# Moving the low products of each half chunk of weights behind the high products of the next half chunk

## The chip, the cores and the metric

The kernel runs on one core of one Trainium2 chip. The metric is the device time of one execution in microseconds (us). The engines are named as the profile names them: PE (TensorE, the matrix products), PEld (its weight loads), DVE (VectorE), ACT (ScalarE), POOL (GpSimd), SP (SyncE, which issues most of the DMAs here). "L201" is line 201 of the kernel before.

## The reference

One layer of a hybrid encoder block on a sequence of 256 tokens with 2048 channels, all in float32. Cut to what matters:

```python
mod = silu(c) @ W_ada + b_ada                        # six vectors of 2048
h = rms_norm(x) * (1 + scale_m) + shift_m
proj = h @ w_in                                       # 2048 x 18512: mLSTM q,k,v,o; GDN q,k,v,z; merge gates
h_a = bidirectional(mlstm_chunkwise, ...)             # 4 heads
o_b = bidirectional(gated_delta_chunkwise, ...)       # 16 heads
y_a = (sigmoid(a_o) * rms_norm(h_a)) @ w_branch_a
y_b = (rms_norm(o_b) * silu(b_z)) @ w_branch_b
x = x + gate_m * ((g_a * y_a + g_b * y_b) @ w_out)
hf = rms_norm(x) * (1 + scale_f) + shift_f
gt, up = split(hf @ w_gate_up)                        # 2048 x 11264
x = x + gate_f * ((silu(gt) * up) @ w_down)           # 5632 x 2048
return rms_norm(x)
```

Nearly all of the work is a product of 256 tokens with a large matrix of weights, each weight being used once.

## The kernel before

**Three products for one.** The large products are taken with operands of type fp32r, and each operand is split in two: a high part, which is the value written as fp32r, and a low part, which is the value minus the high part. A product x·w is then computed as xh·wh + xl·wh + xh·wl. The first two products need only the high part of the weights (in this document: the *high products*), the third needs the low part (the *low products*). The activations are split once and kept (hh and hl, hfh and hfl, and so on). The weights are split as they come in.

**Jobs.** Two generators make all of these products. `fjob` (names b and a) multiplies one block of 2048 x 128 weights; the weights are the stationary operand, and 256 tokens stream past them. `tjob` (names z, v, o, ma, mb, yb, ya, o again for the output projection, gt, up, d) makes 512 output columns for both halves of the tokens; the tokens are the stationary operand, and 512 columns of weights stream past them. A chunk of weights, 1 MB, is brought by one DMA of SP into a tile `raw`. It is converted in two halves: ACT writes `wh` (L155, L180), then DVE writes `wl = raw - wh` (L156, L181). The tiles raw, wh and wl have three buffers each, which all jobs share, and so do the loads of `ada`, 1 MB each, which DVE reduces to the vectors of `mod` (L124) between other work.

**One half chunk on PE.** In `tjob` a half chunk is two blocks of 128 rows times two halves of the tokens, with three products each: twelve products of 128x512. In `fjob` it is eight blocks with three products each: 24 products of 128x256. Before the change the three products of one block follow each other: L199, L200, L201 (L159, L160, L161 in `fjob`), and the third is the low product.

**What sets the order.** The program is written as generators that are interleaved by hand: `fill(n)` advances a list of waiting jobs by n steps, a step being one half chunk, and `stream` and the tables `after` and `last` say how many steps are put between two steps of the gated-delta-rule chain (`gdn_phase2`), so that PE has work while DVE and ACT finish a link of that chain. The links that the prediction speaks of: L685 writes p, DVE makes pt of it (L686), L694 uses pt; then L707, L708 and L719 in the same way. A scheduler then orders the instructions of each engine by this written order and by its own idea of when operands and buffers are ready; a few are marked to stay in written order. Every engine then runs its own list strictly in order, and waits where an operand is missing. A tile's buffer can be written again once its last reader is done: so `wh` is free after the half chunk's last high product, `wl` after its last low product, and `raw` after both halves have been converted.

**Stages, by the time of the span:** to 137 us the modulation and the first 16 column blocks (not split, L507); from 137 to 1000 us the jobs z, v, mb, o, ma, a and b beside the gated delta rule; to 1226 us the mLSTM with yb and ya; to 1334 us the output projection (o again, from the weights `wo`); to 1360 us the second norm with the first gate job; then the gate and up jobs to 1811 us, and the down jobs (d).

## Time and profile before

| | before |
|---|---|
| median of 3 runs | 2050.77 us (2050.05 to 2060.24) |
| the profiled execution | 2056.24 us, its span 2054.3 us |
| PE busy | 1968.2 us (96%) |
| DVE busy | 1394.8 us (68%) |
| ACT busy | 1054.0 us (51%) |
| products | 10374 |
| DMA | 485.64 MB, mean 236 GB/s |

The span is the time from the first to the last instruction that the profile holds; 1.9 us of the execution lie around it. The profiled execution is one run, 5.5 us above the median. A row of the view of waits reads "who waited, at which line, for which engine's which line: us in total, how often, the longest". A row of the timeline has the start in us from the span's beginning, the duration, the engine, the line, what was written from what, and in brackets the idle time before it with what ended it. In the rows by stretch the busy time of each engine stands with the number of its instructions, and then the share of full speed that TensorE's clock was granted.

### The profile page before, as it was taken

The numbers are of one execution on the slowest core, as the hardware profiler recorded it, in microseconds if no ns is written. First come the engines' busy times: TensorE is split into PE (matmuls) and PEld (weight loads), VectorE is DVE, ScalarE is ACT, GpSimd is POOL, SyncE is SP. The second block draws the span as 40 slices with busy tenths as digits, with TensorE's granted clock in tenths as the row PEclk, the third lists the DMA queues.
The fourth block names the chain that finished last, engine by engine and source line by source line (L and its number), as shares of the span: only waits on it lengthen the run. The fifth ranks groups of instructions, "written<-read, shape, count | busy, mean of one in ns | idle before, by whom it ended". The sixth has DMA issues, their size and how long they took to land.

```text
span 2054.3 us, 27035 instructions
## 1 busy us (share of the span) xinstructions
PE 1968.2 (96%) x10374; PEld 1707.0 (83%) x10374; DVE 1394.8 (68%) x2059; ACT 1054.0 (51%) x1584; POOL 106.1 (5%) x205
## 2 busy tenths in 40 slices
PE   8999989999998899999999999889999999999998
PEld 6777779988987898899878787678888888888886
DVE  5787777786888588765667778766656665555554
ACT  3147547856774677466443443364444444444443
POOL 0002210010101010100200000000000000000000
PEclk9999999999999999999999999999999999999999
DMA  9986664566765565666987578756766766555654
GB/s 400 420 321 211 173 216 146 173 190 221 240 224 178 194 207 211 232 247 241 361 295 263 211 264 315 271 184 240 255 243 245 254 238 221 192 204 204 205 203 143
DMA packets 78962, 485.64 MB, mean 236 GB/s; under 512 B 10585, under 2 KB 15969, under 8 KB 24433
## 3 DMA queue, kind: packets, MB, share of 16 engines
q1 hardware_dynamic: 63360, 450.95, 60.9%
q0 software_dynamic: 8160, 17.88, 4.0%
q10 hardware_dynamic: 7314, 15.10, 1.9%
q8 instruction: 81, 1.33, 0.3%
q14 instruction: 47, 0.39, 0.0%
HBM read 467.07 MB, written 16.82 MB: 236 GB/s over the span
## 4 chain that ended last, share of the span: by engine, by line
PE 67%; DVE 13%; DMA 11%; ACT 5%; issue 3%; POOL 1%; ACTq 0%; SPq 0%; DVEq 0%; POOLq 0%
PE acc_up L201 4%; PE acc_up L199 4%; PE acc_up L200 4%; PE acc_d L200 4%; PE acc_d L201 4%; PE acc_d L199 4%; PE acc_gt L200 3%; PE acc_gt L201 3%; PE acc_gt L199 3%; DMA ra<-ada 3%; PE acc_b L161 2%; PE acc_b L159 2%; PE acc_b L160 2%; DMA ada<-ada 2%; PE acc_yb L201 1%
## 5 line engine op out<-in xcount | busy, mean ns | idle before, releaser
L181 DVE TENSOR_TENSOR wl_d<-raw_d,wh_d 128x1024 fp32r<-128x1024 f32 x88 | 107.8, 1225 | 109.1 <-ACT wh_d L180 109.1
L181 DVE TENSOR_TENSOR wl_up<-raw_up,wh_up 128x1024 fp32r<-128x1024 f32 x88 | 107.7, 1225 | 100.4 <-ACT wh_up L180 100.4
L159 PE MATMUL acc_b<-hh,wh_b 128*128 128x256 f32 x576 | 164.1, 285 | 5.8 <-ACT wh_b L155 5.8
L181 DVE TENSOR_TENSOR wl_gt<-raw_gt,wh_gt 128x1024 fp32r<-128x1024 f32 x88 | 107.8, 1225 | 83.2 <-ACT wh_gt L180 83.2
L161 PE MATMUL acc_b<-hh,wl_b 128*128 128x256 f32 x576 | 161.7, 281 | 2.0 <-DVE wl_b L156 2.0
L124 DVE SCALAR_TENSOR_TENSOR ada<-ada,crow 128x2048 f32<-128x2048 f32 x64 | 146.4, 2287 | 25.0 <-DMA ada<-ada 24.8
L160 PE MATMUL acc_b<-hl,wh_b 128*128 128x256 f32 x576 | 160.4, 279 | 0.0
L180 ACT ACTIVATE wh_d<-raw_d 128x1024 fp32r<-128x1024 f32 x88 | 92.9, 1056 | 127.9 <-PE acc_d L200 119.2
L180 ACT ACTIVATE wh_gt<-raw_gt 128x1024 fp32r<-128x1024 f32 x88 | 92.9, 1056 | 118.6 <-PE acc_gt L200 71.0
L180 ACT ACTIVATE wh_up<-raw_up 128x1024 fp32r<-128x1024 f32 x88 | 92.9, 1055 | 108.9 <-PE acc_up L200 78.2
L199 PE MATMUL acc_gt<-wh_gt,hfh 128*128 128x512 f32 x352 | 135.4, 385 | 0.0
L200 PE MATMUL acc_gt<-wh_gt,hfl 128*128 128x512 f32 x352 | 134.7, 383 | 0.1
L201 PE MATMUL acc_gt<-wl_gt,hfh 128*128 128x512 f32 x352 | 133.7, 380 | 0.0
L199 PE MATMUL acc_up<-wh_up,hfh 128*128 128x512 f32 x352 | 133.5, 379 | 0.0
L201 PE MATMUL acc_up<-wl_up,hfh 128*128 128x512 f32 x352 | 133.5, 379 | 0.0
L200 PE MATMUL acc_up<-wh_up,hfl 128*128 128x512 f32 x352 | 133.5, 379 | 0.0
L200 PE MATMUL acc_d<-wh_d,ffl 128*128 128x512 f32 x344 | 131.0, 381 | 0.0
L199 PE MATMUL acc_d<-wh_d,ffh 128*128 128x512 f32 x344 | 131.0, 381 | 0.0
L201 PE MATMUL acc_d<-wl_d,ffh 128*128 128x512 f32 x344 | 130.5, 379 | 0.0
L507 PE MATMUL first<-x,raw 128*128 128x256 f32 x512 | 114.5, 382 | 7.4 <-ACT x L500 6.8
L159 PEld LDWEIGHTS acc_b<-hh,wh_b 128*128 128x128 f32 x576 | 112.5, 195 | 6.4 <-ACT wh_b L155 6.3
L507 PEld LDWEIGHTS first<-x,raw 128*128 128x128 f32 x512 | 96.1, 190 | 25.8 <-ACT x L500 12.4
(369 smaller groups left out, 5275.9 us busy)
## 6 DMA issues: line engine op xcount, KB each, us to landing
ada<-ada SPq DMA_DIRECT2D x64, 1024.0 KB, 5.0
raw_gt<-wgu SPq DMA_DIRECT2D x44, 1024.0 KB, 5.0
raw_up<-wgu SPq DMA_DIRECT2D x44, 1024.0 KB, 4.9
raw_d<-wd SPq DMA_DIRECT2D x44, 1024.0 KB, 4.9
raw_b<-winb SPq DMA_DIRECT2D x36, 1024.0 KB, 5.4
ra<-ada SPq DMA_DIRECT2D x32, 1025.0 KB, 15.7
raw<-win SPq DMA_DIRECT2D x16, 1024.0 KB, 14.5
raw_z<-wint SPq DMA_DIRECT2D x16, 1024.0 KB, 5.8
```

What stands on the lines that cost most here:

```text
L124: V.scalar_tensor_tensor(raw, raw, 1.0, row_c[:, :D], ALU.mult, ALU.mult, accum_out=mod[:, c0 + b : c0 + b + 1])
L159: PE.matmul(o, wh[:, k], both(hh, kk).rearrange("p a b -> p b a"), start=kk == 0, stop=False)
L160: PE.matmul(o, wh[:, k], both(hl, kk).rearrange("p a b -> p b a"), start=False, stop=False)
L161: PE.matmul(o, wl[:, k], both(hh, kk).rearrange("p a b -> p b a"), start=False, stop=kk == KB - 1)
L180: order(S.activation(wh, raws[u][:, k0 : k0 + 2], AF.Copy), early)
L181: order(V.tensor_tensor(wl, raws[u][:, k0 : k0 + 2], wh.bitcast(F32), ALU.subtract), early)
L199: order(PE.matmul(ps[t], tok(xh, kk, t), turns(wh[:, k]), start=kk == 0, stop=False), early and steps > 1)
L200: PE.matmul(ps[t], tok(xl, kk, t), turns(wh[:, k]), start=False, stop=False)
L201: PE.matmul(ps[t], tok(xh, kk, t), turns(wl[:, k]), start=False, stop=kk == last)
L507: PE.matmul(first[o], raw[:, o], x[:, b], start=b == 0 and o % 2 == 0, stop=b == KB - 1 and o % 2 == 1)
```

## The change

The products stay the same, each with the same operands into the same accumulator; their order on PE changes. A half chunk now issues its high products first and puts its low products on a list. The list is emptied down to one entry after the next half chunk's high products, so that the low products of half n stand behind the high products of half n+1. At the end of a job the list is emptied wholly: the last half's high products are followed by the low products of the last two halves. In `fjob`, which has two halves, the order becomes high, high, low, low. The last chunk of the jobs that end token half by token half (`by_token`) has all its high products first and then its low ones. DVE's and ACT's instructions are the same; the scheduler's order of them shifts.

```diff
@@ fjob
+        late = []
         for k0 in range(0, KB, 8):
             ...
             S.activation(wh, raw[:, k0 : k0 + 8], AF.Copy)
             V.tensor_tensor(wl, raw[:, k0 : k0 + 8], wh.bitcast(F32), ALU.subtract)
+            def lows(k0=k0, wl=wl):
+                for k in range(8):
+                    PE.matmul(o, wl[:, k], both(hh, k0 + k).rearrange("p a b -> p b a"), start=False, stop=k0 + k == KB - 1)
+
             for k in range(8):
-                kk = k0 + k
-                PE.matmul(o, wh[:, k], both(hh, kk).rearrange("p a b -> p b a"), start=kk == 0, stop=False)
-                PE.matmul(o, wh[:, k], both(hl, kk).rearrange("p a b -> p b a"), start=False, stop=False)
-                PE.matmul(o, wl[:, k], both(hh, kk).rearrange("p a b -> p b a"), start=False, stop=kk == KB - 1)
+                for i, x in enumerate((hh, hl)):
+                    PE.matmul(o, wh[:, k], both(x, k0 + k).rearrange("p a b -> p b a"), start=k0 + k + i == 0, stop=False)
+            late.append(lows)
+            while len(late) > (not k0):
+                late.pop(0)()
@@ tjob
         for n, (u, k0) in enumerate(todo):
             wh, wl = made.pop(0) if made else halves(u, k0)
-            for k in range(2):
-                kk = 4 * u + k0 + k
-                for t in range(2):
-                    order(PE.matmul(ps[t], tok(xh, kk, t), turns(wh[:, k]), start=kk == 0, stop=False), early and steps > 1)
-                    PE.matmul(ps[t], tok(xl, kk, t), turns(wh[:, k]), start=False, stop=False)
+            kt = [(4 * u + k0 + k, k, t) for k in range(2) for t in range(2)]
+
+            def lows(kt=kt, wl=wl):
+                for kk, k, t in kt:
                     PE.matmul(ps[t], tok(xh, kk, t), turns(wl[:, k]), start=False, stop=kk == last)
+
+            for kk, k, t in kt:
+                order(PE.matmul(ps[t], tok(xh, kk, t), turns(wh[:, k]), start=kk == 0, stop=False), early and steps > 1)
+                PE.matmul(ps[t], tok(xl, kk, t), turns(wh[:, k]), start=False, stop=False)
+            late.append(lows)
+            while len(late) > (n < len(todo) - 1):
+                late.pop(0)()
@@ by_token
-                    wh, wl = (turns(a[:, k % 2]) for a in w[k // 2])
+                    wh = turns(w[k // 2][0][:, k % 2])
                     PE.matmul(ps[t], tok(xh, kk, t), wh, start=False, stop=False)
                     PE.matmul(ps[t], tok(xl, kk, t), wh, start=False, stop=False)
-                    PE.matmul(ps[t], tok(xh, kk, t), wl, start=False, stop=kk == last)
+                for k in range(4):
+                    kk = last - 3 + k
+                    PE.matmul(ps[t], tok(xh, kk, t), turns(w[k // 2][1][:, k % 2]), start=False, stop=kk == last)
```

What the built programs show at three places (the line numbers of the changed kernel differ: L206 is the low product of `tjob`, L209 and L210 its high products, L164 and L160 the high and the low products of `fjob`, L708 is the old L694, L666, L670 and L671 the old L652, L656 and L657, L187 the old L181).

PE, a merge-gate job (ma), chunk 2, second half; the pair of numbers after "ma" in a weight's name is the chunk and the half. Before:

```order
L200 MATMUL acc_ma_1_3458<-wh_ma_2_0_3774,hl 128x512
L201 MATMUL acc_ma_1_3458<-wl_ma_2_0_3775,hh 128x512
L199 MATMUL acc_ma_0_3457<-wh_ma_2_2_3796,hh 128x512
L200 MATMUL acc_ma_0_3457<-wh_ma_2_2_3796,hl 128x512
L201 MATMUL acc_ma_0_3457<-wl_ma_2_2_3797,hh 128x512
L199 MATMUL acc_ma_1_3458<-wh_ma_2_2_3796,hh 128x512
```

With the change:

```order
L206 MATMUL acc_ma_1_3458<-wl_ma_1_2_3749,hh 128x512
L209 MATMUL acc_ma_0_3457<-wh_ma_2_2_3792,hh 128x512
L210 MATMUL acc_ma_0_3457<-wh_ma_2_2_3792,hl 128x512
L209 MATMUL acc_ma_1_3458<-wh_ma_2_2_3792,hh 128x512
L210 MATMUL acc_ma_1_3458<-wh_ma_2_2_3792,hl 128x512
...
L206 MATMUL acc_ma_0_3457<-wl_ma_2_0_3771,hh 128x512
L206 MATMUL acc_ma_1_3458<-wl_ma_2_0_3771,hh 128x512
```

The first low product of half 2_2 was the third product of that half; now the eight high products of 2_2 are followed by the low products of 2_0, and those of 2_2 stand behind the high products of 3_0.

PE, the first pair of heads of the gated delta rule, between the two links L685 and L694, filled by the first half of a b job. Before:

```order
L159 MATMUL acc_b_0_2141<-hh,wh_b_0_0_2144 128x256
L160 MATMUL acc_b_0_2141<-hl,wh_b_0_0_2144 128x256
L161 MATMUL acc_b_0_2141<-hh,wl_b_0_0_2145 128x256
L694 MATMUL p_0_0_2172<-R,pt_0_0_2131 128x32 x4
L159 MATMUL acc_b_0_2141<-hh,wh_b_0_8_2187 128x256
```

With the change:

```order
L164 MATMUL acc_b_0_2137<-hl,wh_b_0_0_2140 128x256
L708 MATMUL p_0_0_2160<-R,pt_0_0_2127 128x32 x4
L164 MATMUL acc_b_0_2137<-hh,wh_b_0_8_2175 128x256
L164 MATMUL acc_b_0_2137<-hl,wh_b_0_8_2175 128x256
...
L160 MATMUL acc_b_0_2137<-hh,wl_b_0_0_2141 128x256 x8
L160 MATMUL acc_b_0_2137<-hh,wl_b_0_8_2176 128x256 x8
```

Where 24 products stood between the two links, 16 stand now; the eight low products moved behind the second half, whose step holds 32 products now instead of 24.

DVE, just ahead of that place, where the blocks of the inverse arrive (cg) and R is made of them. Before:

```order
L652 STREAM_TRANSPOSE cg_1960<-cg_1960 128x512
L656 TENSOR_SCALAR R<-cg_1960,cst 128x256
L181 TENSOR_TENSOR wl_o_2_0_2115<-raw_o_2_2112,wh_o_2_0_2114 128x1024
L657 SCALAR_TENSOR_TENSOR R<-cg_1960,cst,R 128x256
...
L156 TENSOR_TENSOR wl_b_0_0_2145<-raw_b_0_2142,wh_b_0_0_2144 128x1024
```

With the change:

```order
L666 STREAM_TRANSPOSE cg_1956<-cg_1956 128x512
L670 TENSOR_SCALAR R<-cg_1956,cst 128x256
L671 SCALAR_TENSOR_TENSOR R<-cg_1956,cst,R 128x256
L670 TENSOR_SCALAR R<-cg_1956,cst 128x256
L187 TENSOR_TENSOR wl_o_2_0_2111<-raw_o_2_2108,wh_o_2_0_2110 128x1024
...
L157 TENSOR_TENSOR wl_b_0_0_2141<-raw_b_0_2138,wh_b_0_0_2140 128x1024
```

The low part of that half of o moved behind the first pair of instructions that make R, and on PE its low products moved behind the b jobs of this pair of heads.

More of the change, by code (lines that the diff above doesn't have):

```diff
@@ L184, in tjob @@
         todo = [(u, k0) for u in range(len(chunks)) for k0 in (0, 2)]
-        made = []
+        made, late = [], []
         for i, q in enumerate(todo[:early]):
```

## The prediction

> **What bounds the kernel now.** I read the engines' shares first, then the stretches, then who PE waited for, then the timeline around the longest of those waits.
>
> ```profile
> PE 1968.2 (96%) x10374; PEld 1707.0 (83%) x10374; DVE 1394.8 (68%) x2059; ACT 1054.0 (51%) x1584; POOL 106.1 (5%) x205
> ```
>
> PE is busy for 1968.2 of 2054.3 us, so a change of order, which leaves the number of products as it is, can only touch the 86 us between, and what the products themselves lose when the clock drops. Where those 86 us lie is told by the stretches (PE, PEld, DVE, ACT, POOL, then the granted clock and the DMA's share):
>
> ```profile
> 137.00:300.00 163.00, 152.40 (x673) 125.59 (x672) 130.04 (x268) 99.93 (x154) 29.87 (x55) 0.97 0.65 202
> 300.00:620.00 320.00, 305.59 (x2150) 279.75 (x2149) 246.33 (x496) 228.26 (x431) 33.62 (x67) 0.99 0.61 197
> 1226.00:1334.00 108.00, 96.04 (x408) 76.71 (x406) 84.20 (x104) 42.05 (x61) 0.00 (x0) 0.96 0.81 302
> 1360.00:1811.00 451.00, 450.94 (x2120) 392.22 (x2119) 268.57 (x248) 203.30 (x216) 0.00 (x0) 1.00 0.66 236
> ```
>
> In the gate and up jobs PE is never idle (450.94 of 451.00), so that fifth of the kernel has nothing to win. The idle time is in the mixed stages: 10.6 us from 137 to 300, 14.4 us from 300 to 620, and 12.0 us in the output projection. PE's waits on the jobs' operands, and on two links of the gated-delta chain (in total, how often, the longest):
>
> ```profile
> PE acc_o L201 <- DVE wl_o L181: 8.3, 5, 3.3
> PE acc_v L201 <- DVE wl_v L181: 5.1, 5, 2.4
> PE acc_z L201 <- DVE wl_z L181: 4.4, 6, 1.2
> PE acc_ma L201 <- DVE wl_ma L181: 3.7, 2, 2.0
> PE acc_a L161 <- DVE wl_a L156: 2.7, 3, 1.5
> PE acc_b L161 <- DVE wl_b L156: 2.0, 4, 0.8
> PE acc_mb L201 <- DVE wl_mb L181: 0.3, 1, 0.3
> PE acc_b L159 <- ACT wh_b L155: 5.8, 3, 2.8
> PE acc_o L199 <- ACT wh_o L180: 4.0, 5, 1.9
> PE acc_z L199 <- ACT wh_z L180: 2.6, 3, 1.9
> PE p L719 <- DVE pt L708: 2.2, 3, 1.0
> PE p L694 <- DVE pt L686: 2.2, 3, 1.1
> ```
>
> The first seven rows are what the change aims at: the low part of the weights is late, 26.5 us in 26 waits. The next three, 12.4 us in 11 waits, are waits on the high part, which the change leaves in place. One of the first kind, close up:
>
> ```profile
> 451.17 0.38 PE L199 MATMUL acc_ma<-wh_ma,hh 128*128 128x512 f32 x1
> ...
> 455.06 1.06 ACT L180 ACTIVATE wh_ma<-raw_ma 128x1024 fp32r<-128x1024 f32 x1 [1.50 <-PE acc_ma L200]
> 455.30 0.38 PE L200 MATMUL acc_ma<-wh_ma,hl 128*128 128x512 f32 x1
> 456.08 0.40 DVE L631 TENSOR_TENSOR utmp<-uu 64x240 f32<-64x240 f32 x1
> 456.40 1.21 DVE L181 TENSOR_TENSOR wl_ma<-raw_ma,wh_ma 128x1024 fp32r<-128x1024 f32 x1
> 457.67 0.48 PE L201 MATMUL acc_ma<-wl_ma,hh 128*128 128x512 f32 x1 [1.99 <-DVE wl_ma L181]
> ```
>
> From 451.17 to 455.30 PE starts a product every 0.217 us (20 products, 19 steps). At 455.30 it has done the first two products of half 2_2, and the third needs a low part that DVE, busy inverting, begins at 456.40. The other high products of this half could have run, for their operand is there. From start to start the stall costs 2.37 us instead of 0.22, that is 2.15: 0.16 more than the 1.99 of the row, because the idle time counts only from the modelled end of the product before.
>
> **The change part by part.** *The cover.* A half chunk's eight high products take 8 x 0.217 = 1.7 us. Behind the change a low part may come one such block later without PE stopping, in mid-job. Of the 26.5 us I take off:
>
> - 3.9 us, three waits in the output projection. There the loads set the pace, not DVE:
>
> ```profile
> ACT wh_o L180 <- DMA raw_o<-wo: 31.5, 8, 6.1
> 1264.10 2.36 DVE L181 TENSOR_TENSOR wl_o<-raw_o,wh_o 128x1024 fp32r<-128x1024 f32 x2 [1.46 <-ACT wh_o L180]
> L201 PE MATMUL acc_o<-wl_o,mgh 128*128 128x512 f32 x120 | 46.8, 403 | 4.4 <-DVE wl_o L181 3.9
> ```
>
> - 2.1 us, two waits of z, in a stretch in which DVE has 21.80 of 23 us of work, so that PE only reaches the next late operand sooner:
>
> ```profile
> 137.00:160.00 23.00, 21.80 (x42) 1.00 0.57 200
> 148.08 0.70 PE L201 MATMUL acc_z<-wl_z,hh 128*128 128x512 f32 x2 [0.83 <-DVE wl_z L181]
> 152.18 0.70 PE L201 MATMUL acc_z<-wl_z,hh 128*128 128x512 f32 x2 [1.24 <-DVE wl_z L181]
> ```
>
> - 3.3 us, the longest wait of o, priced by itself below.
> - 2.0 us, the four of b: the same job also waits for its high part (5.8 us in the eighth row), so the high products that should cover are not there.
> - 1.0 us, the parts of the longest v (2.4) and ma (2.0) waits beyond the 1.7 us of cover.
> - 0.8 us: the last half of a job has only the four low products before its own as cover, 4 x 0.217 = 0.9 us, and one ma wait of 1.68 us stands there.
>
> 13.4 us are left, in 16 waits (26 less 3, 2, 1 and 4), each with its 0.16 us beside: 13.4 + 2.6 = 16.0 us. The bounds are nothing (PE meets the same lag a block later) and the whole, 26.5 + 26 x 0.16 = 30.7 us.
>
> *The 3.3 us of o* end at the first pair of heads:
>
> ```profile
> 305.74 0.71 DVE L652 STREAM_TRANSPOSE cg<-cg 128x512 f32<-128x512 f32 x1 [7.26 <-DMA cg<-inv_d]
> 307.88 0.48 PE L201 MATMUL acc_o<-wl_o,hh 128*128 128x512 f32 x1 [3.33 <-DVE wl_o L181]
> 308.29 2.00 ACT L155 ACTIVATE wh_b<-raw_b 128x1024 fp32r<-128x1024 f32 x2
> 312.64 0.36 PE L159 MATMUL acc_b<-hh,wh_b 128*128 128x256 f32 x1
> ```
>
> DVE's list stands behind a DMA (cg) for 7.26 us, and the low part of o behind that. With the change PE goes on to the link L685, which waits for R, and then to b, whose high part is there when ACT's first conversion ends, 308.29 + 1.0 = 309.3. Before, b began at 312.64. 3.3 us earlier, less the four low products still owed (0.9): 2.4 us. Bounds: 0 and 3.3.
>
> *The clock.* Behind such stalls the rows show the granted clock at half for 3.4 or 6.8 us (the windows chosen to fit):
>
> ```profile
> 219.50:226.30 6.80, 6.56 (x19) 5.57 (x20) 3.69 (x12) 3.04 (x8) 0.40 (x1) 0.50 0.73 145
> 226.30:233.10 6.80, 6.80 (x28) 5.04 (x27) 3.26 (x4) 2.11 (x2) 0.00 (x0) 1.00 0.57 212
> 458.50:461.80 3.30, 3.30 (x9) 2.59 (x8) 3.20 (x7) 0.60 (x1) 0.08 (x1) 0.50 0.94 308
> ```
>
> At full clock 28 products begin in 6.8 us, at half clock 19, and 9 in 3.3 us: 6.8 x (1 - 19/28) = 2.2 us lost behind the stall of v at 218, and 3.3 - 9 x 6.8/28 = 1.1 us behind that of ma at 457.67. I take 2 of these 3.3 us as won, since another wait stands just before the first one. Bounds: 0 and 3.3.
>
> The Trainium skill (TensorE: Matmul & The Clock Gate, section "HAM oscillation — how this bites in real kernels") states that idle gaps of PE up to about 3.4 us do not drop the clock. By that rule these 2 us would not be won and the gain would be 2 us less; the trace disagrees, since the row at 458.50 stands at 0.50 behind 1.99 us of idle time.
>
> *The chain's cover.* The first half of a b job between L685 and L694 loses its eight low products. Products of `fjob` begin 0.11 us apart:
>
> ```profile
> 312.83 0.28 PE L160 MATMUL acc_b<-hl,wh_b 128*128 128x256 f32 x1
> 312.94 0.28 PE L161 MATMUL acc_b<-hh,wl_b 128*128 128x256 f32 x1
> ```
>
> So the cover falls from 24 x 0.11 = 2.6 to 1.8 us. Where PE waited there already, three times (L694, 2.2 us), the wait grows by 0.9 each: 2.6 us lost. The later step holds 32 products, and of the three waits at L719 the first, up to 1.0, shrinks by 0.9. At the last group's first pair the filling between the second and third application of the inverse shrinks from nine products of 128x512 to one, 1.7 us, of which I count 1.2. Together 2.6 + 1.2 - 0.9 = 2.9 us lost. Bounds: 0.9 won (DVE comes earlier everywhere) and 8 links x 0.9 + 1.7 = 8.9 lost.
>
> *Buffers.* `wh` comes free earlier by the low products that no longer stand before its last reader; `wl` is freed one half later, 12 x 0.217 = 2.6 us, and `raw` with it where DVE then has to wait for a buffer. In mid-job two of three low buffers hold the waiting halves. I cost it at nothing: where loads are late, PE has used up what it had, and the row at 1264.10 shows DVE making both low parts (2.36 us) as soon as ACT is done, with buffers free. Bounds in the third rival. The jobs of 1360 to 1811 stay at nothing, since no operand is late there.
>
> The sum: 16.0 + 2.4 + 2.0 - 2.9 = 17.5 us. The profiled execution took 2056.24 us (span 2054.3 and 1.9 around it), which gives 2038.7; against the median of the runs, 2050.77, it gives **2033 us**.
>
> **Rivals.** *The lag only moves.* DVE is late because its list is full for a stretch (130.04 of 163 us, 21.80 of 23 at its start). The cover then pays once per stretch and not once per wait: the stretches of z and v, ma, z with a, o with a make about five, 5 x 1.7 = 8.5 us, less the chain's 2.9: some 6 us, 2045 us, within what a measurement can tell from no change (0.5%, about 10 us). For it: the waits of z come in a row. Against it: over each long stretch DVE has a fifth of its time free, and most waits stand alone.
>
> *The chain loses what the jobs win.* All eight links stall (7.2 and 1.7 us), and each new stall brings a piece of half clock like that at 458.50 (1.1 us): 8.9 + 8 x 1.1 = 17.7 us against 20.4 won: 2048 us. Against it: five of the eight links show no wait, so their cover had something to spare.
>
> *Buffers held longer.* If a low buffer kept for one more half delays raw's release and so the next load by 2.6 us, the 11 waits on high parts (12.4 us, loads already late) grow by 2.6 each: 28.6 us against 17.5 won, 11 us slower: 2062 us. It decides from the point at which DVE waits for a buffer and no longer for ACT before it writes a low part, in stages where the loads are just in time. For it: b jobs run while another job is paused with a low part pending, which leaves them two buffers. Against it: the row at 1264.10.
>
> That the change does not do what it says is excluded by the order: the low products stand behind the next half's high ones.
>
> **How the numbers follow.** My forecast 0.57; the lag only moves 0.23; the chain 0.05; buffers 0.13; the last 0.02 for other shifts of the scheduler that cost time. Faster by over 0.5% (below about 2040) only in the first: 0.57; within 0.5% in the second and third: 0.28; slower 0.15. The forecast's own range runs from the whole of the cover with nothing lost, 2050.8 - 30.7 - 3.3 + 2.9 = 2020, to 2040. The range that should hold the time 8 times in 10 takes in both cases of no change and the start of the slower one: 2019 to 2055.
>
> **What would show it.** Right: the seven rows of PE behind DVE's low parts fall from 26.5 to about 9 us, mostly in the output projection; no stall at 457.67, and no half clock behind it; L694 waits about 2.6 us longer; 1360 to 1811 unchanged. The forecast is wrong if waits on wh grow by what the waits on wl lose (the lag moved, or late loads), or if ACT's waits on loads grow by some 2.6 us each.

## The result, and the profile after

The changed kernel takes 2062.64 us (median of 20 runs, 2056.23 to 2072.60) against 2054.22 us of the kernel before on the same chip (20 runs, 2046.72 to 2060.24). The ratio is 1.0045, with an interval of 1.0033 to 1.0057: 9.2 us slower. That lies within the 0.5% that the prediction set as the bound of "no change", but it is clear of zero, and far from the 17.5 us that were forecast as won.

The engines, in the profiled execution of the changed kernel (span 2070.6 us, the execution 2072.6, which is the slowest of its 20 runs; so its stages may be longer than the typical ones):

```profile
PE 1975.9 (95%) x10374; PEld 1720.2 (83%) x10374; DVE 1392.5 (67%) x2059; ACT 1040.5 (50%) x1578; POOL 106.1 (5%) x205
```

PE idles 94.7 us, where it idled 86 before. The view by stretches, cut at the stages: up to the first product of yb, then the output projection, then from its end to that of the first gate job. First the three rows of the kernel before, then those of the changed one. The columns are the bounds, the length, PE, PEld, DVE, ACT, POOL, the granted clock, the DMA's share and GB/s:

```profile
0.00:1016.90 1016.90, 961.37 (x5742) 849.53 (x5743) 751.25 (x1366) 593.29 (x1039) 104.00 (x201) 0.98 0.69 240
1225.60:1328.70 103.10, 94.51 (x401) 75.42 (x399) 81.33 (x96) 39.49 (x53) 0.00 (x0) 0.97 0.85 316
1328.70:1365.50 36.80, 27.84 (x130) 22.61 (x130) 23.92 (x40) 26.23 (x47) 0.00 (x0) 0.95 0.33 115
```

```profile
0.00:1011.70 1011.70, 957.80 (x5742) 853.53 (x5743) 749.68 (x1366) 581.76 (x1031) 103.97 (x201) 0.98 0.69 242
1221.80:1338.30 116.50, 98.28 (x401) 79.06 (x399) 82.14 (x97) 38.27 (x52) 0.00 (x0) 0.91 0.76 280
1338.30:1381.60 43.30, 33.84 (x133) 26.55 (x133) 23.71 (x40) 26.09 (x47) 0.00 (x0) 0.84 0.29 98
```

Up to yb the change wins 5.2 us. Then it loses 13.4 us in the output projection (116.5 against 103.1) and 6.5 us in the second norm with the first gate job (43.3 against 36.8), and in both the clock is lower (0.91 for 0.97, 0.84 for 0.95). The other gate and up jobs take 445.7 us against 445.8, the down jobs 243.3 against 243.0.

Who PE waited for, after:

```profile
PE acc_o L209 <- ACT wh_o L186: 12.0, 5, 4.4
PE acc_b L164 <- ACT wh_b L156: 8.0, 7, 3.0
PE row L1086 <- DVE dg L1084: 6.1, 1, 6.1
PE acc_z L209 <- ACT wh_z L186: 5.6, 2, 5.1
PE acc_ma L206 <- DVE wl_ma L187: 3.9, 1, 3.9
PE acc_v L206 <- DVE wl_v L187: 3.5, 3, 2.5
PE acc_a L160 <- DVE wl_a L157: 2.6, 3, 1.9
PE acc_z L206 <- DVE wl_z L187: 1.6, 1, 1.6
PE p L708 <- DVE pt L700: 1.3, 2, 0.9
PE p L733 <- DVE pt L722: 0.9, 1, 0.9
```

The waits on low parts (L206, L160) fell as meant, from 26.5 to 11.6 us. But the waits of o, b and z on *high* parts grew from 12.4 to 25.6 us (12.0 + 8.0 + 5.6), and a wait of 6.1 us is new: PE at the row product L1086, for DVE's dg. The two links of the gated-delta chain (the last two rows; L694 and L719 before) wait less, 2.2 us instead of 4.4.

The reason shows not on PE but on DVE. The groups of the low parts of ya, o and d with all that ended DVE's idle time ahead of them (busy and mean ns, then the idle time and its causes), first before, then after:

```profile
L181 DVE TENSOR_TENSOR wl_o<-raw_o,wh_o 128x1024 fp32r<-128x1024 f32 x64 | 76.8, 1218 | 28.7 <-ACT wh_o L180 27.7 <-PE acc_o L201 0.9
L181 DVE TENSOR_TENSOR wl_ya<-raw_ya,wh_ya 128x1024 fp32r<-128x1024 f32 x32 | 39.1, 1223 | 24.4 <-ACT wh_ya L180 24.2
```

```profile
L187 DVE TENSOR_TENSOR wl_d<-raw_d,wh_d 128x1024 fp32r<-128x1024 f32 x88 | 107.8, 1225 | 108.6 <-PE acc_d L206 103.9 <-PE acc_up L206 2.7 <-issue 2.0
L187 DVE TENSOR_TENSOR wl_o<-raw_o,wh_o 128x1024 fp32r<-128x1024 f32 x64 | 76.8, 1220 | 33.3 <-PE acc_o L206 14.3 <-ACT wh_o L186 11.9 <-PE acc_ya L206 2.7
L187 DVE TENSOR_TENSOR wl_ya<-raw_ya,wh_ya 128x1024 fp32r<-128x1024 f32 x32 | 38.9, 1223 | 24.9 <-PE acc_ya L206 17.0 <-ACT wh_ya L186 4.9 <-PE acc_yb L206 2.9
```

Before, DVE waited for ACT, that is, for its input. After, it waits in ya mostly, and in o in part, for PE's low products: for a free low buffer. (The 64 low parts of o are 32 of the early jobs and 32 of the output projection; in the stretch of the projection alone, 9.3 us of DVE's idle time end with PE's acc_o.) The idle time itself is nearly the same (24.9 for 24.4 in ya), but it ends at another event, and DVE holds everything behind it back until then. In the down jobs 103.9 us of such waits cost next to nothing (243.3 us for 243.0). At three places they cost more.

**The start of the output projection.** `ada` is one of the loads for the vectors of `mod`, `x` the 2 MB of the residual; dg of the gate row needs the sum over `ada`. The timeline before, then after:

```profile
1225.30 0.33 SPq L123 DMA_DIRECT2D ada<-ada  x1
1225.76 0.34 ACTq L1062 DMA_DIRECT2D x<-xr  x1
1230.34 2.29 DVE L124 SCALAR_TENSOR_TENSOR ada<-ada,crow 128x2048 f32<-128x2048 f32 x1
```

```profile
1221.18 1.23 DVE L187 TENSOR_TENSOR wl_o<-raw_o,wh_o 128x1024 fp32r<-128x1024 f32 x1 [1.38 <-PE acc_ya L206]
1221.97 0.34 ACTq L1076 DMA_DIRECT2D x<-xr  x1
1222.44 0.33 SPq L123 DMA_DIRECT2D ada<-ada  x1
1233.47 2.29 DVE L124 SCALAR_TENSOR_TENSOR ada<-ada,crow 128x2048 f32<-128x2048 f32 x1 [5.95 <-DMA ada<-ada]
1237.90 1.19 PE L1086 MATMUL row<-dg,ones 128*128 128x512 f32 x1 [6.09 <-DVE dg L1084]
```

The low part at 1221.18 waits 1.38 us for a buffer that the last ya products still hold. It frees the raw tile, and SP's list issues `ada` behind that. Against the projection's first product (1225.56 before, 1221.78 after) `ada` is issued at +0.66 us instead of -0.26, and `x` at +0.20 both times. So `ada` goes from 0.46 us ahead of the 2 MB load to 0.47 us behind it, and lands 11.0 us after its issue (1222.44 to 1233.47) instead of 5.0 (1225.30 to 1230.34). DVE stands at L124 for 5.95 us, and PE for 6.09 behind it. A shift of 0.9 us has become a wait of 6.

**Within the projection** DVE waits for low buffers too, the longest time here:

```profile
1245.33 1.23 DVE L187 TENSOR_TENSOR wl_o<-raw_o,wh_o 128x1024 fp32r<-128x1024 f32 x1 [4.53 <-PE acc_o L206]
```

The tile raw_o stays occupied that long, and the loads behind it start later.

**The first gate job.** It is made block by block with the second norm, and has two low parts made ahead and one pending, which is all three buffers. One block, before and then after:

```profile
1342.68 1.23 DVE L181 TENSOR_TENSOR wl_gt<-raw_gt,wh_gt 128x1024 fp32r<-128x1024 f32 x1 [0.52 <-ACT wh_gt L180]
1344.40 0.42 ACT L1174 ACTIVATE hfh<-hf 128x256 fp32r<-128x256 f32 x1 [1.75 <-DVE hf L1173]
```

```profile
1353.80 1.22 DVE L187 TENSOR_TENSOR wl_gt<-raw_gt,wh_gt 128x1024 fp32r<-128x1024 f32 x1 [2.21 <-PE acc_gt L206]
1354.95 0.54 DVE L1187 TENSOR_SCALAR hf<-pxn,affn,mod 128x256 f32<-128x256 f32 x1
1355.52 0.42 ACT L1188 ACTIVATE hfh<-hf 128x256 fp32r<-128x256 f32 x1 [3.44 <-DVE hf L1187]
```

On DVE's list the low part stands ahead of the norm's own step hf. It waits 2.21 us for a buffer, hf waits behind it, and ACT's hfh, which PE needs for the next block, waits 3.44 us instead of 1.75. Why the buffer is late here is told by the clock, in the stretch ahead of it and the next one:

```profile
1345.90:1349.30 3.40, 1.44 (x8) 0.82 (x8) 3.01 (x5) 2.88 (x5) 0.00 (x0) 1.00 0.35 80
1349.30:1352.70 3.40, 3.40 (x11) 2.65 (x10) 1.33 (x3) 2.23 (x4) 0.00 (x0) 0.50 0.55 229
```

PE is busy for 1.44 of 3.40 us, between two blocks, and in the next 3.40 us its clock is granted at half, with 11 products begun. The low products that free the buffer come that much later.

### The profile page after: what moved, and what is told of

It is laid out like the page before. It is cut to its first block, busy times and chain, and to the rows that moved or that the text cites. A ratio compares the mean times of both kernels' runs of the same rounds, so it can differ in the third digit from the quotient of the medians.

```text
span 2070.6 us, 27069 instructions
## 1 busy us (share of the span) xinstructions
PE 1975.9 (95%) x10374; PEld 1720.2 (83%) x10374; DVE 1392.5 (67%) x2059; ACT 1040.5 (50%) x1578; POOL 106.1 (5%) x205
## 4 chain that ended last, share of the span: by engine, by line
PE 49%; DMA 4%; DVE 2%; issue 1%; ACT 1%; POOL 0%; ACTq 0%; DVEq 0%; POOLq 0%
PE acc_up L210 4%; PE acc_up L209 4%; PE acc_d L210 4%; PE acc_up L206 4%; PE acc_d L206 4%; PE acc_d L209 4%; PE acc_gt L210 4%; PE acc_gt L209 4%; PE acc_gt L206 4%; PE acc_yb L209 1%; PE acc_yb L210 1%; PE acc_yb L206 1%; PE acc_ya L206 1%; PE acc_ya L210 1%; PE acc_ya L209 1%
## 5 line engine op out<-in xcount | busy, mean ns | idle before, releaser
L187 DVE TENSOR_TENSOR wl_d<-raw_d,wh_d 128x1024 fp32r<-128x1024 f32 x88 | 107.8, 1225 | 108.6 <-PE acc_d L206 103.9
L187 DVE TENSOR_TENSOR wl_up<-raw_up,wh_up 128x1024 fp32r<-128x1024 f32 x88 | 106.7, 1224 | 102.6 <-PE acc_up L206 72.5
L187 DVE TENSOR_TENSOR wl_gt<-raw_gt,wh_gt 128x1024 fp32r<-128x1024 f32 x88 | 107.7, 1224 | 85.7 <-PE acc_gt L206 54.2
L124 DVE SCALAR_TENSOR_TENSOR ada<-ada,crow 128x2048 f32<-128x2048 f32 x64 | 146.4, 2287 | 23.3 <-DMA ada<-ada 23.0
L164 PE MATMUL acc_b<-hh,wh_b 128*128 128x256 f32 x576 | 141.8, 290 | 8.3 <-ACT wh_b L156 8.0
L210 PE MATMUL acc_gt<-wh_gt,hfl 128*128 128x512 f32 x352 | 138.9, 395 | 0.0
L209 PE MATMUL acc_gt<-wh_gt,hfh 128*128 128x512 f32 x352 | 137.7, 391 | 0.1
L164 PE MATMUL acc_b<-hl,wh_b 128*128 128x256 f32 x576 | 137.7, 284 | 0.0
L210 PE MATMUL acc_up<-wh_up,hfl 128*128 128x512 f32 x352 | 133.6, 379 | 0.0
L209 PE MATMUL acc_up<-wh_up,hfh 128*128 128x512 f32 x352 | 133.5, 379 | 0.0
L210 PE MATMUL acc_d<-wh_d,ffl 128*128 128x512 f32 x344 | 130.7, 380 | 0.0
L209 PE MATMUL acc_d<-wh_d,ffh 128*128 128x512 f32 x344 | 130.5, 379 | 0.0
L164 PEld LDWEIGHTS acc_b<-hh,wh_b 128*128 128x128 f32 x576 | 115.0, 200 | 9.5 <-ACT wh_b L156 9.1
L164 PEld LDWEIGHTS acc_b<-hl,wh_b 128*128 128x128 f32 x576 | 115.0, 200 | 0.0
L157 DVE TENSOR_TENSOR wl_b<-raw_b,wh_b 128x1024 fp32r<-128x1024 f32 x72 | 85.8, 1220 | 38.5 <-PE acc_b L160 19.4
L186 ACT ACTIVATE wh_o<-raw_o 128x1024 fp32r<-128x1024 f32 x64 | 65.6, 1051 | 78.9 <-DMA raw_o<-wo 40.5
L310 DVE SCALAR_TENSOR_TENSOR cv<-pad,pk,cv 128x256 f32<-128x256 f32 x192 | 90.8, 481 | 14.6 <-ACT cv L308 12.5
```

The lines of the kernel that those rows point to most:

```text
L124: V.scalar_tensor_tensor(raw, raw, 1.0, row_c[:, :D], ALU.mult, ALU.mult, accum_out=mod[:, c0 + b : c0 + b + 1])
L157: V.tensor_tensor(wl, raw[:, k0 : k0 + 8], wh.bitcast(F32), ALU.subtract)
L164: PE.matmul(o, wh[:, k], both(x, k0 + k).rearrange("p a b -> p b a"), start=k0 + k + i == 0, stop=False)
L186: order(S.activation(wh, raws[u][:, k0 : k0 + 2], AF.Copy), early)
L187: order(V.tensor_tensor(wl, raws[u][:, k0 : k0 + 2], wh.bitcast(F32), ALU.subtract), early)
L209: order(PE.matmul(ps[t], tok(xh, kk, t), turns(wh[:, k]), start=kk == 0, stop=False), early and steps > 1)
```

## The experiments

The theory after the result: the new order wins some us up to yb, and from yb on a low buffer kept a half longer loses more than that, at the three places above. The rivals: the new order is slower everywhere because the clock drops more often; or the loss comes from one accident alone, the load of `ada` behind that of `x`. All ratios are against the kernel before on the same chip, with a 95% interval. The changed kernel was not run again beside these kernels, so what one of them wins back is the distance of its ratio from 1.0045, and that distance is uncertain by some 4 to 6 us.

**Each half of the program alone.** In both, `old` puts each low product where it stood before:

```diff
+            old = xh is not hh        # late half alone: "xh is hh", with fjob as before
...
                 PE.matmul(ps[t], tok(xl, kk, t), turns(wh[:, k]), start=False, stop=False)
-            late.append(lows)
+                if old:
+                    PE.matmul(ps[t], tok(xh, kk, t), turns(wl[:, k]), start=False, stop=kk == last)
+            if not old:
+                late.append(lows)
```

The new order only up to yb:

> The new order only in the jobs up to 1000 us (b, a, z, v, the output gate o, ma, mb); yb, ya, the output projection, gate, up and down in the old order. Theory A (held buffers: the loss lies behind 1000 us, because a low buffer that is kept one half longer delays raw's release and the loads from there on, most of all at the start of the output projection): the lead of the profile of the changed kernel, 5.2 us at the first product of yb, is kept, so 5 to 8 us below the kernel before, about 2046 to 2049 us. Theory B (clock: the short waits that are gone are balanced by fewer but longer ones that halve the clock, wherever they lie): within 3 us of the kernel before, granted clock at or below 0.984.

The new order only from yb on:

> The new order only from yb on (yb, ya, the output projection, gate, up and down); fjob and the jobs up to 1000 us in the old order. Theory A: the whole loss without the gain, 10 to 14 us above the kernel before, 2064 to 2068 us, with the load of ada behind the 2 MB load of x1 at the start of the output projection and PE waiting some 6 us for dg there. Theory B: within 3 us of the kernel before.

Measured: 0.9969 (0.9948 to 0.9990; 2048.72 us, 12 runs) for the early half and 1.0069 (1.0053 to 1.0086; 2070.90 us, 6 runs) for the late one. The two add up to 1.0038, near the 1.0045 of the whole change. So the early half wins about 6 us and the late half loses about 14. A drop of the clock everywhere is out as the main cause: the early half alone is faster than before. That rests on the twelve runs: the profiled one of the early half is among its slowest (2059.92 us), and reaches yb only at 1020.3 us.

**The load of x.** In the first try its line was moved behind the second gate row:

```diff
-    S.dma_start(x1, xr)
...
     row(2, gm, wp)
+    S.dma_start(x1, xr)
```

> The changed kernel with one line moved: the 2 MB load of x1 is written behind the first gate row and not ahead of it, so that it can't be in front of the load of ada. Theory A: ada lands about 5 us after its issue and not 11, PE's wait of 6.1 us for dg goes, 6 us below the changed kernel, about 2056 us; the rest of the loss (later loads within the projection) stays. If the 6.1 us are a slip of the one profile: no change, about 2062 us.

Measured: 1.0046 (1.0030 to 1.0062; 2064.39 us, 6 runs). This says nothing of the cause: the scheduler issued the load where it had been, 0.20 us behind the projection's first product. The second try makes the load depend on that row, by a copy of one column into its target:

```diff
+            if part == 2 and g == 1:
+                S.activation(x1[:, 0, 0:1], dst[:, 512:513], AF.Copy)
+                S.dma_start(x1, xr)
```

> The changed kernel with the 2 MB load of x1 made to wait for the second gate row (a one-column copy of that row into x1 goes ahead of the load), so that it is issued some 8 us later, behind the load of ada. (In the run x1late the line's place in the program did not move the load: it was still issued 0.20 us behind the projection's first product, 0.46 us ahead of ada's.) If the two loads' order causes the wait for dg: ada lands about 5 us after its issue, PE's wait for dg falls from 6.1 to under 1.5 us, and the ratio to the kernel before falls from 1.0045 to about 1.002. If the projection is paced by its later loads anyway: the wait goes, the ratio stays at 1.0045.

Measured: 1.0023 (0.9999 to 1.0048; 2059.66 us, 10 runs). The issue of `ada` in this kernel, DVE's sum over it, and its sum over the next one:

```profile
1214.71 0.33 SPq L123 DMA_DIRECT2D ada<-ada  x1
1223.63 2.28 DVE L124 SCALAR_TENSOR_TENSOR ada<-ada,crow 128x2048 f32<-128x2048 f32 x1
1236.03 2.29 DVE L124 SCALAR_TENSOR_TENSOR ada<-ada,crow 128x2048 f32<-128x2048 f32 x1 [8.77 <-DMA ada<-ada]
```

`ada` is issued as late as in the changed kernel, 0.66 us behind the first product (at 1214.05), but DVE no longer waits for it, and PE's wait at the row product is gone. So it was the load of x ahead of it that made that wait. But x, issued at 1223.18 now, comes ahead of the next load of `ada`, and DVE waits 8.77 us for that one: the collision has moved. The projection still takes 113.3 us. The median ratio falls by 0.0022, about 4.6 us, but the intervals overlap, and in the profile it is the first gate job, which the edit does not concern, that is 5 us shorter (below). What the place of this load is worth in time is not settled by this run.

**The old order in one place at a time.** The line `old` of above, with `name[:2] == "ya"`, `name == "gt0"`, or the output projection alone.

> The changed kernel with the old order in the four ya jobs alone. If the low buffer held one half longer in ya is what delays ada's load: DVE's last low part before the projection waits for ACT again and not for PE's low products, ada is issued about 0.27 us ahead of the projection's first product and ahead of x1's load, lands in 5 us, and the wait for dg goes: ratio about 1.002. If the scheduler's order has another cause: ada still behind x1, 1.0045.

> The changed kernel with the old order in the first gate job alone. In the profiles this stage (from the projection's last product to the first up product) takes 40.1 us with the new order and 12 products fewer than the 36.7 us before. If the order costs it: 3 to 5 us below the changed kernel, ratio 1.002 to 1.003, and fewer pieces of half clock there than four. If those pieces fell there by chance: 1.0045.

> The changed kernel with the old order in the output projection alone (four jobs). Theory A: the low buffers of ya are still held longer, so ada's load still falls behind x1's and the 6 us stay, but the loads within the projection come about 0.5 us sooner per chunk (16 chunks, 12 of them paced by loads): 4 to 6 us below the changed kernel, about 2057 us. If the order within the projection does the whole damage: 10 to 13 us below, about 2050 us. If it does none: about 2062 us.

Measured: ya 0.9996 (0.9972 to 1.0019; 2055.64 us, 10 runs), the first gate job 1.0031 (1.0012 to 1.0050; 2061.85 us, 10 runs), the output projection 1.0012 (0.9999 to 1.0026; 2058.96 us, 12 runs). Against 1.0045 that is 10, 3 and 7 us won back. The 10 and the 7 are clear of the uncertainty, the 3 are not: for the gate job the stage in the profiles has to tell. The row of `ada` with the old order in ya, then the projection with the old order in the projection, and the first gate job with the old order there:

```profile
1216.59 0.33 SPq L123 DMA_DIRECT2D ada<-ada  x1
1221.84 2.29 DVE L124 SCALAR_TENSOR_TENSOR ada<-ada,crow 128x2048 f32<-128x2048 f32 x1 [0.17 <-DMA ada<-ada]
```

```profile
1218.60:1326.40 107.80, 93.77 (x401) 73.64 (x399) 82.00 (x97) 38.65 (x52) 0.00 (x0) 0.97 0.82 302
```

```profile
1332.30:1369.90 37.60, 30.84 (x130) 24.76 (x130) 23.99 (x40) 26.31 (x47) 0.00 (x0) 0.86 0.32 112
```

With the old order in ya, `ada` is issued 0.26 us ahead of the projection's first product again, lands in 5.2 us, and DVE waits 0.17 us for it: the order of the products in one job decides when a load of the next stage is issued. The projection, in the new order still, takes 109.0 us there. With the old order in the projection instead, it falls from 116.5 to 107.8 us with `ada` still late (DVE waits 5.2 us for it). The first gate job is back at 37.6 us, from 43.3.

What goes on in the gate job is told by a run that did not aim at it. In the kernel with the load of x tied behind the gate row, the first gate job has the new order and takes 38.2 us. The same place there: the low part of the second block, and the two stretches that answer to those shown above (between two blocks, and the next):

```profile
1341.09 1.23 DVE L187 TENSOR_TENSOR wl_gt<-raw_gt,wh_gt 128x1024 fp32r<-128x1024 f32 x1 [0.52 <-ACT wh_gt L186]
```

```profile
1335.80:1339.20 3.40, 1.88 (x10) 1.38 (x10) 2.58 (x5) 2.40 (x5) 0.00 (x0) 1.00 0.68 193
1339.20:1342.60 3.40, 3.40 (x20) 2.98 (x19) 2.36 (x4) 1.83 (x4) 0.00 (x0) 1.00 0.28 116
```

PE is busy for 1.88 of the 3.40 us between the blocks, the clock stays whole (20 products in the next 3.40 us, not 11), and DVE waits for ACT as before the change. So the kept buffer costs little here as long as the clock stays whole. It costs where the clock has dropped: then the low products are late, DVE holds hf back, two blocks take 10.2 us instead of 8.5, and in the gap of every second block the clock drops again. In the changed kernel the half-clock pieces stand at 1342.5, 1349.3, 1359.6 and 1369.8; in this one there is a single one, at 1332.4. Over the profiles with the new order in this job it took 43.3, 43.3, 43.3, 43.0, 41.7, 40.2 and 38.2 us, over those with the old order 36.7 to 37.6, though the clock fell once or twice there as well.

**More buffers instead.** The new order everywhere, with four low buffers that belong to the output projection alone:

```diff
+            four = name[0] == "o" and xh is not hh
+            lp = lowp["p"] if four else st
-            wl = st.tile([P, 2, 512], F32R, tag="wl", bufs=3, ...)
+            wl = lp.tile([P, 2, 512], F32R, tag="wl4" if four else "wl", bufs=4 if four else 3, ...)
```

> The changed kernel, but the output projection's low parts have four buffers of their own instead of sharing three. If buffers held longer are what makes the projection's loads late: DVE's waits for PE's low products go from that stage, raw comes free earlier, and the stage shrinks by 3 to 6 us like with the old order there (ratio 1.0015 to 1.003). If the order on PE itself is what costs (finished low parts behind high products whose operand has not come): no change, 1.0045.

The same four buffers in the kernel before, as a control:

> The kernel before, whole, with four low buffers of their own in the output projection; nothing is left out. If DVE waits there for ACT and not for a buffer, as the trace of before says, a fourth buffer alone changes little: ratio 0.998 to 1.001, the projection at 101 to 104 us. Rival (the kernel before is short of low buffers in the projection too, and the run with four buffers under the new order owes its time to that): some 5 us faster, 0.9975 or less, the projection under 99 us.

Measured: 0.9998 (0.9978 to 1.0017; 2054.96 us, 10 runs) with the new order, 1.0005 (0.9990 to 1.0021; 2056.56 us, 12 runs) in the kernel before. The projections of the two:

```profile
1213.30:1315.90 102.60, 91.95 (x401) 74.86 (x399) 83.78 (x98) 38.19 (x52) 0.00 (x0) 0.98 0.85 317
```

```profile
1224.50:1326.20 101.70, 92.65 (x401) 74.55 (x399) 83.70 (x98) 39.73 (x53) 0.00 (x0) 0.98 0.86 320
```

Four buffers of its own take 13.9 us off the projection of the changed kernel (116.5 to 102.6), where 3 to 6 were expected, and nothing that can be measured off the kernel before. DVE waits for no low buffer in that projection any more. But that is not all that the edit did: `ada` is issued at 1221.30 there, 8.0 us behind the projection's first product and after x has landed, so the two loads do not meet either. The run takes both losses away at once and does not part them.

**The new order only where it pays.** The old order in ya, the output projection and the first gate job, the new one elsewhere; and the same with the new order and four buffers in the projection:

```diff
+            old = name[:2] == "ya" or name == "gt0" or name[0] == "o" and xh is not hh   # the first
+            old = name[:2] == "ya" or name == "gt0"                                      # the second, with the four buffers
```

> The old order stands in ya, in the output projection and in the first gate job, the new one in all others; nothing is left out. Theory (low buffers kept a half longer cost time in these three places, and the new order wins some 8 us before 1000 us): ratio to before about 0.996, some 8 us faster, as with the new order early alone, since yb, the other gate and up jobs and the down jobs are neutral; the output projection takes about 103 us, the first gate job about 37, DVE does not wait for ada at the third gate row. Rival (a lower granted clock over the whole kernel, which goes with the new order wherever it is, makes the loss): 1.000 or more.

> The old order in ya and in the first gate job, the new one everywhere else, and in the output projection four low buffers that belong to it alone; nothing is left out. Theory: the new order in the projection is then free of its buffer and wins there what it was to win, 0 to 3 us: ratio 0.994 to 0.997, the projection at 102 to 104 us. Rival (the four buffers only bring the projection back to what it was): the same time as with the old order in all three places.

Measured: 0.9941 (0.9921 to 0.9962; 2043.60 us, 6 runs) and 0.9979 (0.9964 to 0.9994; 2053.48 us, 12 runs). The first beats the kernel before by about 12 us and the changed one by about 21: three conditions on the order turn the loss into a gain. The 21 us are about what the three places brought back one by one (10 + 7 + 3). That is more than the 14 us that the late half alone lost; whether yb and the other jobs win the difference, or it is the spread of the ratios, was not settled. Its stages (to yb, the projection, the first gate job):

```profile
0.00:1004.30 1004.30, 955.89 (x5742) 849.98 (x5743) 748.79 (x1364) 581.75 (x1031) 103.95 (x201) 0.98 0.70 243
1208.30:1310.00 101.70, 93.42 (x401) 74.31 (x399) 81.55 (x96) 39.69 (x53) 0.00 (x0) 0.98 0.87 320
1310.00:1347.50 37.50, 29.49 (x129) 23.73 (x130) 24.00 (x40) 26.21 (x47) 0.00 (x0) 0.91 0.33 113
```

The second was expected to be the better one, with the projection at 102 to 104 us, and is not. Its projection, and PE's waits in it, then those of the first:

```profile
1217.10:1327.20 110.10, 95.06 (x401) 77.13 (x400) 83.65 (x98) 39.30 (x53) 0.00 (x0) 0.95 0.82 296
PE acc_o L214 <- ACT wh_o L190: 14.9, 7, 4.6
```

```profile
PE acc_o L213 <- DVE wl_o L187: 4.0, 3, 2.3
PE acc_o L210 <- ACT wh_o L186: 3.5, 5, 1.6
```

With the four buffers the new order removes the waits on low parts there (4.0 us, as L213) and adds more on high parts (14.9 against 3.5). The projection is 8.4 us longer than in the first (110.1 against 101.7), about what the ratios differ by. DVE waits for a low buffer for only 1.9 us of it. With the old order in ya and three buffers the projection took 109.0 us, with the new order in ya and four it took 102.6. So in the new order the fourth buffer is not enough by itself, and the shortage of low buffers is not the whole of what the projection loses. What else it is stays open: one profile of each kernel does not tell the place of the loads from the spread between executions. That going ahead, in a stage that the loads pace, only meets the next load sooner would fit the rows, but no run tests it.

**The early half without a and b.** `fjob` as before, the new order in the jobs z, v, o, ma and mb only:

> The new order in the jobs z, v, o, ma and mb alone; the old one in a and b and in all jobs from yb on; nothing is left out. Theory (the chain's cover in b costs 2.9 us, as forecast): faster than with a and b changed as well, by some 3 us: ratio about 0.9955. Rival (the cover of b had enough to spare, or its gain pays for it): the same ratio as with a and b changed, 0.997, or above it.

Measured: 0.9991 (0.9975 to 1.0006; 2055.87 us, 12 runs), where 0.9955 was expected; with a and b changed it was 0.9969. The wait that stands in its place:

```profile
PE acc_b L161 <- DVE wl_b L156: 5.5, 8, 1.3
```

Before it was 2.0 us in 4 waits; with a and b changed there is none. So by these rows the change in b does not cost its cover, it catches a lag that the other jobs pass on. The intervals of 0.9991 and 0.9969 overlap. The stage up to yb points the same way: 1015.2 us here, 1011.9 to 1016.9 in the three profiles with the old order in all the early jobs, and a median of 1007.6 over the ten with the new order in all of them (1002.7 to 1020.3, the longest being that of the early half alone).

## Why the prediction was wrong

The step that failed is the one on buffers: "I cost it at nothing". The third rival named the mechanism and the point from which it decides, DVE waiting for a buffer and no longer for ACT, and that is what the rows of wl_o and wl_ya show. Its price, 2062 us, happens to fit the median too, but not by its sum. It let 11 waits on high parts grow by 2.6 us each. What was paid, by the ratios, is the order of ya (10 us; in the profile the wait of 6.1 us behind the late load goes and the projection takes 7.5 us less, and the rest was not taken apart), the order within the projection (7, of which DVE's waits for low buffers are a part that was not measured by itself) and the first gate job (3; 5.7 in the profiles, 43.3 against 37.6), where the kept buffer lets the clock drop again and again. The evidence that I set against this rival, the row at 1264.10, was taken from where loads are late. It does not tell of ya just before, where DVE keeps up and takes the last free buffer. The sign that the prediction named for this case, ACT's waits on loads, would not have told either: those on the projection's loads grew from 31.5 to 40.5 us, but they stand at 42.3 in the kernel with the old order in three places, whose projection takes 101.7.

Point by point:

- *The cover.* Right in kind: the seven rows fell from 26.5 to 11.6 us (about 9 was said, mostly in the output projection; none of the 11.6 lie there), the stall at 457.67 went, and PE came sooner to what follows. Too large in size: of 17.5 us in all, the early half alone brought about 6. The named sign that the lag had moved was there, waits on high parts growing, of b (5.8 to 8.0) and z (2.6 to 5.6) in this half. By these rows PE's waits on low parts fell by 11.0 us in this half (22.6 to 11.6) and those on high parts grew by 6.3 (b and z 5.2, mb and a 1.1), which leaves 4.7. So more than half of the lag only moved, as the first rival said ("the lag only moves", about 6 us).
- *The projection.* Leaving its three waits out of the gain was right: they went (3.9 us), and those on high parts grew from 4.0 to 12.0. That the stage would lose was not seen.
- *The 3.3 us of o.* 2.4 us were forecast; in the changed kernel the first b product starts where the chain's link lets it, at 306.75 instead of 312.64, so more than that was won up to there, and the last pair's first link starts 7.8 us sooner (918.35 for 926.10).
- *The clock.* 2.0 us were to be won. The half-clock pieces amount to 89.8 us within the span after and 56.4 before. If half of each piece is lost, that is (89.8 - 56.4) / 2 = 16.7 us, an estimate. That the two spans differ by as much (16.3) is in part chance: PE's idle time grew by 8.7 us beside it, and its busy time, for the same products, by 7.7. The late stages have most of the pieces that are new: three of 6.8 us in the projection, where there was one, and four of 3.4 us around the first gate job, where there was one. They stand behind the new stalls and make them dearer, and in the gate job they also bring the next one. The kernel with the old order in three places has 54.6 us of them in all. But the total alone does not tell the kernels apart: in the profile of the early half alone it is 82 us, and two thirds of that lie between 137 us and yb.
- *The chain.* 2.9 us were to be lost; its two links wait 2.2 us less, and the kernel without the change in a and b is no better. The term had the wrong sign: of its bounds, the one that was a gain (0.9) came nearer.
- *The jobs of 1360 to 1811.* Right: 445.7 us for 445.8, though DVE waits there for buffers as well. PE has work there whatever DVE does.

Part of the 29.6 us between 2033 and 2062.64 is the yardstick: the median of before was 2050.77 over 3 runs and 2054.22 over 20. The rest is about 17.5 - 6 = 11 us of early gain that was not there and 14 of late loss.

## What to carry to other kernels

An order that keeps a rotating buffer longer changes what the writer waits for, and an engine that works its list in order passes that wait to everything behind it: ask at each end of a stage what stands behind the writer (a release, a load, a step of the next stage), not only whether the consumer has work. Groups that name the releaser show it where the idle time in total does not (24.9 us for 24.4). And an order can be chosen stage by stage: here it paid where the operand was late by the engine's work, and lost where the writer had no free buffer and something that others needed stood behind it.

## What the runs showed of the hardware that was not expected

Two loads on different queues, 1 MB and 2 MB, issued 0.46 us apart, did not share evenly here: the first landed first. Issued ahead, the 1 MB landed after 5.0 us (and the 2 MB after 9.9); issued behind, after 11.0 (and the 2 MB after 9.5). In the other traces with the one order or the other it is the same: 4.9 to 5.2 us ahead, 9.6 to 11.1 behind. In the changed kernel, from the issue of the 1 MB at 1222.44 up to 1226.4, only packets of the other queue moved, 1.20 MB of them. The Trainium skill (DMA: Bandwidth & Descriptors, section "Queues, rings and completion order") states that each DMA engine takes turns between the queues, packet by packet. If even turns began at the issue, the 1 MB would land ahead of the 2 MB also when it is issued second; the trace shows it landing last. Whether the engines took no turns in the first 4 us, or had no packets of the second load to take yet, no run here shows.

The clock goes by windows. In each of the fourteen traces the half-clock pieces begin on one grid of 3.41 us, which lies differently in each execution. Cut along that grid from 137 to 2020 us, a window at full clock in which PE was busy for less than 0.40 of the time was followed by half clock in 106 of 106 cases, one with 0.40 to 0.45 in 37 of 50, one with 0.45 to 0.50 in 6 of 28, one with 0.50 to 0.60 in 18 of 95, and one above 0.60 in 22 of some 7190. The two pairs of rows above show it: 1.44 of 3.40 us (0.42) was followed by 0.50, 1.88 of 3.40 (0.55) by 1.00. The Trainium skill (TensorE: Matmul & The Clock Gate, section "HAM oscillation — how this bites in real kernels") gives "no PE-idle gaps >~3.4µs" as the rule, which the prediction took to clear the shorter ones. The traces agree with that page's window, but a shorter gap is not safe: about 2 us of idle within one window (a busy share of 0.40 to 0.45) were enough in 37 of 50 cases, and cost up to 1.7 us more (half of 3.4) where PE has work throughout the next window. An idle time that the grid splits between two windows counts less in each. That this is why runs of one kernel spread would fit, but is not shown, since each kernel was traced once. What is measured is the clock: over the 20 runs of the changed kernel the mean granted clock lies between 0.978 and 0.986, and the time falls by 1.43 us for each 0.001 of it (correlation -0.82).
